# One transposition of the gated product for both token halves in a two-layer encoder on Trainium2

## The chip, the cores and the metric

The kernel runs on one core of one Trainium2 chip. The metric is the device time of one execution in microseconds; three runs stand for the kernel before. The core's engines run side by side, each with its own queue: TensorE (PE, with its weight loads as PEld), VectorE (DVE), ScalarE (ACT), GpSimd (POOL) and SyncE (SP), which issues the DMAs.

## What is computed

One sequence of 256 tokens with 1024 channels goes through two layers in float32. Each layer has two half-step feed-forward blocks around a mixer of three branches:

```python
def swiglu_ffn(h, w_gate, w_up, w_down):
    return (jax.nn.silu(h @ w_gate) * (h @ w_up)) @ w_down
# each layer:
#   x += 0.5 * SwiGLU(RMSNorm(x))                (ffn1)
#   h  = RMSNorm(x); branches S5, GLA, GQA of one input projection of h,
#   each projected to 1024 and weighted by a sigmoid gate from h, then w_out
#   x += merged
#   x += 0.5 * SwiGLU(RMSNorm(x))                (ffn2)
```

The inner width of the feed-forward block is 2816. S5 is a bidirectional state space model over 32 groups, GLA a gated linear attention with four heads, GQA an attention with eight query heads and two key heads.

## The kernel before

**Matrix products.** Tokens are the 128 stationary rows (two halves, `t` = 0 and 1), weights are the moving 512 columns. For precision each float32 operand is split into a high part `hi` and a low part `lo`, and `mm3` issues three matmuls for each k tile of 128: hi by hi (L219), hi by lo (L220), lo by hi (L221). `load` brings weights by DMA into `raw`, two k tiles in one tile; ScalarE copies them to `hi` (L209) and VectorE subtracts to get `lo` (L210). `hi` and `lo` have rings of four, `raw` one of five, and one part feeds 12 matmuls.

**The feed-forward block.** `ffn` has 2816 / 256 = 11 blocks of 256 inner channels. For a block the gate's 256 columns and the up projection's 256 columns make one 512-column bank for each token half; 48 matmuls fill both. Then `evac(b)` is called for t = 0 and t = 1. It applies silu on ScalarE (L294), multiplies on VectorE (L295), and the product, 128 tokens by 256 channels, is transposed on TensorE, since it is the stationary operand of the down projection: two 128x128 transposes (L298) into one PSUM tile `st` of half a bank. ScalarE copies that to the high part `sTh` (L300) and VectorE subtracts to get the low part `sTl` (L301), 128x256 each. `down` then runs over all 22 k tiles of `sTh` and `sTl`. The scratch ring "ra" has four tiles, the PSUM pool `ptr` two banks.

**Stages.** `run` weaves ffn1 of layer 0 with the S5 tables of that layer (`s5_tables`, mostly VectorE), then comes the mixer, then ffn2 of layer 0 and ffn1 of layer 1 in a chain, woven with the tables of layer 1, then the second mixer, ffn2 of layer 1 alone, and the final norm. In the trace these are 0 to 215, 215 to 490, 490 to 895, 895 to 1188 and 1188 to the end.

**The mixer.** The input projection, three gate streams, three branch projections and the merge are TensorE's main work; S5, GLA and attention are side parts woven into it. S5 runs in four quarters: products with an exponential table on VectorE, four scans (L835, L836), products with the run's sums (L349), and TensorE's outputs `yp` (L853, L856). GLA works a head at a time: scores `sp`, masked with a predicated copy (L988), state `kv`, output `go` and its transposition `goT`. Attention works two heads at a time: scores `as` (L1070), softmax on VectorE and ScalarE, transposed probabilities `apt` (L1085) with a copy (L1087), and the product `ao` (L1092). `as`, `yp`, `sp`, `kv` and `ao` share a PSUM ring of three banks.

**What sets the order.** The program is emitted in Python in woven order, with a priority by which weight parts run ahead. The framework then sets the final order of each engine by a timeline of its own at compile time (`schedule_with_timeline_sim=True`), in which every instruction has an assumed duration. Each engine runs its instructions in that fixed order.

Of the kernel before, what the change touches and what calls it, by code (L numbers as in the profile page):

```python
# [9 lines left out]
F32 = mybir.dt.float32  # L10
# [5 lines left out]
P = 128  # L16
D = 1024
KD = D // P
SEQ = 256
# [19 lines left out]
# main steps before a side part begins, and its steps per main step  # L39
# [12 lines left out]
# columns of the constants: those for the mixer, then those for the tables  # L52
# [4 lines left out]
def constants():  # L57
    """Arrays that depend on shapes alone, one row per partition."""
    c = np.zeros((P, C_ALL), np.float32)
    p = np.arange(P)  # L60
    inv = (10000.0 ** (-np.arange(16, dtype=np.float32) * 2.0 / 32)).astype(np.float32)
    for t in range(NT):
        tok = t * P + p
        for blk, pos in ((0, tok // 64), (1, tok % 64)):
            ang = (pos.astype(np.float32)[:, None] * inv[None]).astype(np.float64)
            for half in range(2):
                o = t * 64 + blk * 32 + half * 16
                c[:, C_COS + o:C_COS + o + 16] = np.cos(ang)
                c[:, C_SIN + o:C_SIN + o + 16] = np.sin(ang) * (1 if half else -1)
    c[:, C_MASK:C_MASK + P] = p[:, None] < p[None]  # L70
    c[:, C_TWO:C_TWO + P] = 1 + np.eye(P)
    i = np.arange(SEQ)
    c[:, C_RST:C_RST + SEQ] = i % P != 0
    n = np.arange(64)
    c[:64, C_RM:C_RM + 64] = n != 0
    c[64:, C_RM:C_RM + 64] = n != 63
    q = p % 32
    c[p, C_DM + q] = 1.0
    c[:, C_SGN] = np.where(p < 64, 1.0, -1.0)
    return c  # L80


def cols(*parts):
    """Columns of weights [K, N] side by side: for the k tiles [a, z)."""
    def f(a, z):
        res, o = [], 0
        for w, cs in parts:
            res.append((w[a * P:z * P, cs].rearrange("(k p) n -> p k n", p=P), 0, o))
            o += cs.stop - cs.start
        return res  # L90
    return f


def weave(main, sides, up=nullcontext):
    """Emit main; from its step `start` on, `per` steps of a side part after each step of main.
    sides: list of [start, per, generator]. Whatever is left of them comes in the end."""
    acc = [0.0] * len(sides)
    for i, _ in enumerate(main):
        for j, (start, per, g) in enumerate(sides):
            if i >= start:  # L100
                acc[j] += per
                while acc[j] >= 1.0:
                    acc[j] -= 1.0
                    with up():
                        next(g, None)
    for _, _, g in sides:
        for _ in g:
            pass


def rest(*gens):
    """Emit what is left of these parts, in turn, as one step."""
    gens = list(gens)
    while gens:
        for g in list(gens):
            if next(g, gens) is gens:
                gens.remove(g)
    yield
# [7 lines left out]
class Enc:  # L126
# [38 lines left out]
    def vectors(self, *names, eng=None):  # L165
        """Parameters of channels, to partitions: [128 channels, (layer, tile)]"""
# [26 lines left out]
    def load(self, pieces):  # L193
        """pieces: list of (dram AP [partitions, k tiles, columns], first partition, first column)"""
# [21 lines left out]
    def mm3(self, ps, act, w, first, last):  # L216
        """act: (hi, lo) [128 k, 128 tok]; w: (hi, lo) [128 k, n]"""
# [5 lines left out]
    def stream(self, act, nk, blocks, lead=1):  # L223
        """act(k, t) -> (hi, lo). blocks: list of (pieces(k0, k1) in k tiles, width, evac(t, ps)).
        The first `lead` blocks take their first chunks together."""
# [55 lines left out]
    def ffn(self, l, which):  # L281
        nc, ins = self.nc, self.ins
        wg, wu, wd = (ins[f"{which}_w_{s}"][l] for s in ("gate", "up", "down"))
        with self.tc.tile_pool(name=f"ffn{which}{l}", bufs=1) as fp:
# [5 lines left out]
            def evac(b):  # L290
                def f(t, ps):
                    self.n += 1
                    sg, s = self.t2([P, 256]), self.t2([P, 256])
                    nc.scalar.activation(sg, ps[:, :256], AF.Silu, scale=rstd[:, t:t + 1])  # L294
                    nc.vector.scalar_tensor_tensor(s, ps[:, 256:], rstd[:, t:t + 1], sg, op0=ALU.mult, op1=ALU.mult)  # L295
                    pt = self.ptr.tile([P, 2, P], F32, name=f"st{self.n}", tag="tr")
                    for j in range(2):
                        nc.tensor.transpose(pt[:, j], s[:, j * P:(j + 1) * P], self.ident)  # L298
                    h = sh[:, 2 * b:2 * b + 2, t * P:(t + 1) * P]
                    nc.scalar.copy(h, pt)  # L300
                    nc.vector.tensor_tensor(sl[:, 2 * b:2 * b + 2, t * P:(t + 1) * P], pt, h.bitcast(F32),  # L301
                                            op=ALU.subtract)
                return f
# [57 lines left out]
    def cmul_steps(self, o_re, o_im, a_re, a_im, b_re, b_im, tmp, neg=False):  # L361
        """o = a * b; with neg, o_im is its negative. tmp: four scratch APs"""
# [13 lines left out]
    def horner(self, out, x, cs):  # L376
        """cs from the highest power down"""
# [6 lines left out]
    def reduce_arg(self, r, n, x, inv, parts):  # L384
        """n = nearest integer of x * inv; r = x - n * (sum of parts)"""
# [40 lines left out]
    def s5_params(self, l, c):  # L426
# [68 lines left out]
        # the first four powers, turned back by a chunk  # L495
# [12 lines left out]
        # ef: powers 0 .. 7 of the turn over a chunk; eg: those of its eighth power  # L508
# [130 lines left out]
    def small_tables(self, l, pp):  # L639
        """What the mixer needs apart from its large weights: half the GLA gain, the padded gate weights with the  # L640
        bias as a last row, the rotary tables with the gains of q and k"""
# [36 lines left out]
    def split_into(self, hi, lo, src):  # L678
        """src -> two float32r parts"""
# [68 lines left out]
    def gate_stream(self, l, i, act, rstd, gates):  # L748
        """The tanh of half the gate's argument: sigmoid(v) = (1 + tanh(v / 2)) / 2"""
# [32 lines left out]
    def s5(self, l, m):  # L782
# [18 lines left out]
        for q in range(NQ):  # L801
# [31 lines left out]
            # sums up to the chunk before (forward: after), nothing at the ends  # L833
# [67 lines left out]
    # ---- gate logits: z in two parts against weights in two parts, the products one above the other:  # L901
    # ---- [high z, 1 | high z, 1 | low z] . [high w, high b | low w, low b | high w]
# [18 lines left out]
    # ---- gated linear attention, both directions, a head at a time, over chunks of 128 tokens; the exponents  # L921
# [1 line left out]
    def gla(self, l, m, y):  # L923
# [26 lines left out]
        for h in range(GH):  # L950
# [34 lines left out]
            # a token's own score is the same both ways: forward ones above the diagonal, twice those on it, backward below  # L985
# [113 lines left out]
    def branch(self, l, b, y, gates):  # L1099
        """Generator bodies run late: y[b] is there by then."""  # L1100
# [76 lines left out]
```

## Time and profile before

| | |
|---|---|
| Median of three runs | 1378.79 us (1378.58 to 1380.41) |
| Profiled execution: span | 1376.2 us |
| TensorE busy | 1336.0 us, 97% |
| VectorE busy | 1018.4 us, 74% |
| ScalarE busy | 698.6 us, 51% |
| GpSimd busy | 73.5 us, 5% |

The profiled execution has only its span, 2.6 us under the median of the runs. Busy time counts instructions, not waits; a matmul's listed duration overlaps with the next one's, so the distance from start to start is what one takes of the engine. "[1.27 <-DVE lo L210]" behind a row means that the engine was idle for 1.27 us before it, and that the last thing it waited for was the tile `lo` of line 210 on VectorE.

### The profile page before, as it was taken

To read this page: it belongs to the slowest core of one execution; us is meant where nothing else is said; L and a number is where in the kernel's file an instruction comes from. 1 tells how busy PE (TensorE), PEld (TensorE's weight loads), DVE (VectorE), ACT (ScalarE), POOL (GpSimd) and SP (SyncE) were. 2 spreads that over 40 slices of the span, in tenths; PEclk is the share of its full clock that TensorE was granted. 3 is DMA by queue.
4 is the path that set the end of the run, shared out by engine and by line. 5 is a ranking of instruction groups with operands and counts; after the bars stand their busy time and mean duration, and the time that the engine had idled before them with its cause. 6 is when DMAs were issued, how large, how long until landed. Compare 5 with 4: busy or idle time off the path is not lost.

```text
span 1376.2 us, 19506 instructions
## 1 busy us (share of the span) xinstructions
PE 1336.0 (97%) x6920; PEld 1061.6 (77%) x6920; DVE 1018.4 (74%) x1826; ACT 698.6 (51%) x1102; POOL 73.5 (5%) x104
## 2 busy tenths in 40 slices
PE   7999999999999999999999999999999999999997
PEld 5878788778787678768877777887787877888886
DVE  5899975779986789996465775457799767655553
ACT  5545345447585355445355454354475754555542
POOL 1020210000100000110000000000001000000000
PEclk9999999999999999999999999999999999999999
DMA  7766666565453366666665646566654533655662
GB/s 227 195 211 224 234 222 179 189 205 198 140 183 122 107 161 206 200 202 221 198 195 173 204 149 204 180 178 202 196 200 134 168 107 122 191 178 186 182 213 76
DMA packets 201201, 249.88 MB, mean 182 GB/s; under 512 B 40856, under 2 KB 134600, under 8 KB 201104
## 3 DMA queue, kind: packets, MB, share of 16 engines
q1 hardware_dynamic: 200496, 247.59, 57.5%
q8 instruction: 54, 0.88, 0.3%
q10 hardware_dynamic: 608, 1.06, 0.2%
q14 instruction: 43, 0.35, 0.1%
HBM read 234.44 MB, written 13.11 MB: 180 GB/s over the span
## 4 chain that ended last, share of the span: by engine, by line
PE 63%; issue 17%; DVE 13%; DMA 3%; ACT 3%; POOL 1%; SPq 0%; POOLq 0%; ACTq 0%; DVEq 0%
PE mm L220 18%; PE mm L219 17%; PE mm L221 17%; DVE lo L210 4%; PE S L818 1%; DMA raw<-in_ffn_w_gate 1%; DMA raw<-in_ffn_w_up 1%; PE as L1070 1%; ACT hi L209 1%; PE ao L1092 1%; DVE t L349 1%; PE st L298 1%; DVE run L836 1%; DVE run L835 1%; PE apt L1085 1%
## 5 line engine op out<-in xcount | busy, mean ns | idle before, releaser
L210 DVE TENSOR_TENSOR lo<-raw,hi 128x1024 fp32r<-128x1024 f32 x412 | 499.4, 1217 | 191.7 <-ACT hi L209 184.1
L209 ACT CAST hi<-raw 128x1024 fp32r<-128x1024 f32 x412 | 427.7, 1042 | 305.6 <-PE mm L221 276.3
L220 PE MATMUL mm<-lo,hTh 128*128 128x512 f32 (+1 forms) x1120 | 445.3, 398 | 5.3 <-DVE lo L210 4.9
L219 PE MATMUL mm<-hi,hTh 128*128 128x512 f32 (+1 forms) x1120 | 437.6, 396 | 2.7 <-ACT hTh L267 2.7
L221 PE MATMUL mm<-hi,hTl 128*128 128x512 f32 (+1 forms) x1120 | 436.1, 392 | 0.0
L220 PEld LDWEIGHTS mm<-lo,hTh 128*128 128x128 f32 x1120 | 211.2, 189 | 51.7 <-DVE lo L210 9.2
L219 PEld LDWEIGHTS mm<-hi,hTh 128*128 128x128 f32 x1120 | 211.2, 189 | 45.5 <-ACT hTh L267 3.8
L221 PEld LDWEIGHTS mm<-hi,hTl 128*128 128x128 f32 x1120 | 210.6, 188 | 40.6 <-DVE hTl L268 0.3
L220 PE MATMUL mm<-lo,sThffn 128*128 128x512 f32 x352 | 138.9, 395 | 2.0 <-DVE lo L210 2.0
L221 PE MATMUL mm<-hi,sTlffn 128*128 128x512 f32 x352 | 138.1, 393 | 0.0
L219 PE MATMUL mm<-hi,sThffn 128*128 128x512 f32 x352 | 136.4, 395 | 0.0
L300 ACT CAST sThffn<-st 128x256 fp32r<-128x256 f32 x88 | 32.6, 372 | 128.7 <-PE st L298 128.5
L220 PEld LDWEIGHTS mm<-lo,sThffn 128*128 128x128 f32 x352 | 66.4, 189 | 16.6 <-DVE lo L210 2.5
L221 PEld LDWEIGHTS mm<-hi,sTlffn 128*128 128x128 f32 x352 | 66.5, 189 | 14.1
L219 PEld LDWEIGHTS mm<-hi,sThffn 128*128 128x128 f32 x352 | 66.5, 189 | 13.8
L301 DVE TENSOR_TENSOR sTlffn<-st,sThffn 128x256 fp32r<-128x256 f32 x88 | 36.9, 421 | 50.3 <-ACT sThffn L300 49.9
L294 ACT ACTIVATE t<-mm,rstd 128x256 f32<-128x256 f32 x88 | 41.6, 475 | 43.0 <-PE mm L221 40.2
L295 DVE SCALAR_TENSOR_TENSOR t<-mm,rstd,t 128x256 f32<-128x256 f32 x88 | 41.4, 479 | 12.6 <-ACT t L294 12.4
L818 PEld LDWEIGHTS S<-U,bb 64*128 64x128 f32 x256 | 24.6, 187 | 12.8 <-issue 11.2
L298 PE MATMUL st<-ident,t 128*128 128x128 f32 x176 | 33.4, 272 | 0.0
L298 PEld LDWEIGHTS st<-ident,t 128*128 128x128 f32 x176 | 24.4, 140 | 11.3
L349 DVE TENSOR_TENSOR t<-e,S 128x256 f32<-128x256 f32 x64 | 22.4, 414 | 12.7 <-DMA e<-scr 6.9
(355 smaller groups left out, 1452.6 us busy)
## 6 DMA issues: line engine op xcount, KB each, us to landing
raw<-in_ffn_w_gate SPq DMA_DIRECT2D x176, 256.0 KB, 3.7
raw<-in_ffn_w_up SPq DMA_DIRECT2D x176, 256.0 KB, 4.4
raw<-in_ffn_w_down SPq DMA_DIRECT2D x88, 512.0 KB, 4.6
raw<-in_w_in SPq DMA_DIRECT2D x48, 512.0 KB, 4.4
raw<-in_w_merge_gate SPq DMA_DIRECT2D x48, 512.0 KB, 3.8
raw<-in_w_out SPq DMA_DIRECT2D x16, 512.0 KB, 4.6
scr<-e SPq DMA_DIRECT2D x6, 768.0 KB, 3.7
e<-scr SPq DMA_DIRECT2D x6, 768.0 KB, 5.7
```

Of the source, the lines that this page charges most:

```text
L209: nc.scalar.copy(hi[:, :e - s, :width], raw[:, :e - s, :width])
L210: nc.vector.tensor_tensor(lo[:, :e - s, :width], raw[:, :e - s, :width], hi[:, :e - s, :width].bitcast(F32), op=ALU.subtract)
L219: nc.tensor.matmul(ps, act[0], w[0], start=first, stop=False)
L220: nc.tensor.matmul(ps, act[0], w[1], start=False, stop=False)
L221: nc.tensor.matmul(ps, act[1], w[0], start=False, stop=last)
L294: nc.scalar.activation(sg, ps[:, :256], AF.Silu, scale=rstd[:, t:t + 1])
L295: nc.vector.scalar_tensor_tensor(s, ps[:, 256:], rstd[:, t:t + 1], sg, op0=ALU.mult, op1=ALU.mult)
L298: nc.tensor.transpose(pt[:, j], s[:, j * P:(j + 1) * P], self.ident)
L300: nc.scalar.copy(h, pt)
L301: nc.vector.tensor_tensor(sl[:, 2 * b:2 * b + 2, t * P:(t + 1) * P], pt, h.bitcast(F32), op=ALU.subtract)
L349: self.nc.vector.tensor_tensor(out, a, b, op=ALU.mult)
L818: nc.tensor.matmul(S[g][:, r, a * 64:(a + 1) * 64], bb[rows, a, r], U[rows, pair[a]], start=True, stop=True)
```

## The change

In `evac` the transposes move from each token half to the second call. The first call only makes the gated product of half 0 and keeps it; the second makes that of half 1, issues four transposes into one full bank `[128, 2, 256]`, and splits the whole with one copy and one subtraction of 128x512, by the helper `split_into` that other places use too. The products of both halves live longer: the ring "ra" of four holds silu and product of both halves, exactly a block's. All else in the diff are comments taken out, which shift nothing but three lines of numbering behind `evac`.

```diff
             def evac(b):
+                s = []
+
                 def f(t, ps):
-                    self.n += 1
-                    sg, s = self.t2([P, 256]), self.t2([P, 256])
+                    sg = self.t2([P, 256])
+                    s.append(self.t2([P, 256]))
                     nc.scalar.activation(sg, ps[:, :256], AF.Silu, scale=rstd[:, t:t + 1])
-                    nc.vector.scalar_tensor_tensor(s, ps[:, 256:], rstd[:, t:t + 1], sg, op0=ALU.mult, op1=ALU.mult)
-                    pt = self.ptr.tile([P, 2, P], F32, name=f"st{self.n}", tag="tr")
-                    for j in range(2):
-                        nc.tensor.transpose(pt[:, j], s[:, j * P:(j + 1) * P], self.ident)
-                    h = sh[:, 2 * b:2 * b + 2, t * P:(t + 1) * P]
-                    nc.scalar.copy(h, pt)
-                    nc.vector.tensor_tensor(sl[:, 2 * b:2 * b + 2, t * P:(t + 1) * P], pt, h.bitcast(F32),
-                                            op=ALU.subtract)
+                    nc.vector.scalar_tensor_tensor(s[t], ps[:, 256:], rstd[:, t:t + 1], sg, op0=ALU.mult, op1=ALU.mult)
+                    if t < NT - 1:
+                        return
+
+                    pt = self.ptr.tile([P, 2, SEQ], F32, name=self.nm("st"), tag="tr")
+                    for i in range(NT):
+                        for j in range(2):
+                            nc.tensor.transpose(pt[:, j, i * P:(i + 1) * P], s[i][:, j * P:(j + 1) * P], self.ident)
+                    self.split_into(sh[:, 2 * b:2 * b + 2], sl[:, 2 * b:2 * b + 2], pt)
                 return f
```

`split_into(hi, lo, src)` is `nc.scalar.copy(hi, src)` and `nc.vector.tensor_tensor(lo, src, hi.bitcast(F32), op=ALU.subtract)`.

All orders below are the fixed ones of the compiled programs; numbers behind names only tell tiles apart, and lines of the changed kernel are three higher behind `evac` (L835 is L838, L1070 is L1073).

In ffn2 of layer 0, VectorE, where the tables of layer 1 are worked out: before, twelve rows that end with the `lo` that TensorE waits for at 600.84 (the `lo` ahead of it, lo_5774, is five rows above the first of them).

```order
L373 TENSOR_TENSOR e_6538<-U_6423,U_6424 128x512
L301 TENSOR_TENSOR sTlffn_4915<-st_5682,sThffn_4914 128x2x128
L364 TENSOR_TENSOR T_6533<-bb_7025,lpb 128x512
L365 TENSOR_TENSOR T_6534<-bb_7025,lpb 128x512
L366 TENSOR_TENSOR T_6535<-bb_7025,lpb 128x512
L301 TENSOR_TENSOR sTlffn_4915<-st_5691,sThffn_4914 128x2x128
L368 TENSOR_TENSOR T_6536<-bb_7025,lpb 128x512
L364 TENSOR_TENSOR U_6421<-ef,eg 128x512
L365 TENSOR_TENSOR U_6422<-ef,eg 128x512
L366 TENSOR_TENSOR U_6423<-ef,eg 128x512
L368 TENSOR_TENSOR U_6424<-ef,eg 128x512
L210 TENSOR_TENSOR lo_5835<-raw_5831,hi_5834 128x1024
```

In the changed kernel, VectorE at the same weight parts:

```order
L368 TENSOR_TENSOR U_6356<-ef,eg 128x512
L369 TENSOR_TENSOR U_6357<-ef,eg 128x512
L372 TENSOR_TENSOR e_6472<-U_6355,U_6356 128x512
L684 TENSOR_TENSOR sTlffn_4882<-st_5635,sThffn_4881 128x512
L376 TENSOR_TENSOR e_6472<-U_6357,U_6358 128x512
L210 TENSOR_TENSOR lo_5778<-raw_5774,hi_5777 128x1024
L367 TENSOR_TENSOR U_6355<-ef,eg 128x512
L368 TENSOR_TENSOR U_6356<-ef,eg 128x512
L210 TENSOR_TENSOR lo_5785<-raw_5781,hi_5784 128x1024
L369 TENSOR_TENSOR U_6357<-ef,eg 128x512
L371 TENSOR_TENSOR U_6358<-ef,eg 128x512
L210 TENSOR_TENSOR lo_5832<-raw_5828,hi_5831 128x1024
```

Weight parts stand three rows apart there; the longest stretch without one in these tables now is ten rows, a little further on, and was fifteen before.

In the mixer of layer 0, VectorE at the last quarter of S5: `run` are the scans, t_3461 the GLA's masked scores, and the memsets set the run's ends. Before:

```order
L835 SCALAR_TENSOR_TENSOR run_2589<-e_3338,t_3363 64x511
L836 SCALAR_TENSOR_TENSOR run_2589<-e_3338,t_3363 64x511
L835 SCALAR_TENSOR_TENSOR run_2589<-e_3338,t_3365 64x511
L836 SCALAR_TENSOR_TENSOR run_2589<-e_3338,t_3365 64x511
L349 TENSOR_TENSOR t_3461<-sp_3534,cst 128x256
L1030 TENSOR_REDUCE ass_3464<-t_3472 128x8
L838 MEMSET run_2589 64x16
L839 MEMSET run_2589 64x16
L210 TENSOR_TENSOR lo_3918<-raw_3915,hi_3917 128x1024
L988 COPY_PREDICATED t_3461<-cst,sp_3534 128x256
L349 TENSOR_TENSOR t_3363<-e_3338,run_2589 128x512
L349 TENSOR_TENSOR t_3365<-e_3338,run_2589 128x512
```

After, from the weight part ahead of the scans on (t_3428 are now the masked scores):

```order
L210 TENSOR_TENSOR lo_3891<-raw_3888,hi_3890 128x1024
L1033 TENSOR_REDUCE ass_3431<-t_3436 128x2
L838 SCALAR_TENSOR_TENSOR run_2556<-e_3305,t_3330 64x511
L839 SCALAR_TENSOR_TENSOR run_2556<-e_3305,t_3330 64x511
L838 SCALAR_TENSOR_TENSOR run_2556<-e_3305,t_3332 64x511
L839 SCALAR_TENSOR_TENSOR run_2556<-e_3305,t_3332 64x511
L764 SCALAR_TENSOR_TENSOR gate_1_3726<-mm_3743,rstd_2328,bm_3727 128x512
L210 TENSOR_TENSOR lo_3988<-raw_3985,hi_3987 128x1024
L352 TENSOR_TENSOR t_3428<-sp_3501,cst 128x256
L1033 TENSOR_REDUCE ass_3431<-t_3439 128x8
L956 SCALAR_TENSOR_TENSOR t_3693<-cst,la_3077 128x256
L957 SCALAR_TENSOR_TENSOR t_3693<-cst,la_3077 128x256
```

Before, the next weight part, lo_3918, stood five rows behind the last scan; now lo_3988 stands two rows behind it. The predicated copy followed lo_3918 directly; now it has left this stretch and follows the weight part after lo_3988.

In the mixer of layer 0, TensorE in the attention's tail. Before:

```order
L1092 MATMUL ao_4073<-t_4016,av_2415 64x256
L1092 MATMUL ao_4073<-t_4000,av_2415 64x256
L1092 MATMUL ao_4073<-t_4016,av_2415 64x256
L1070 MATMUL as_4081<-akT_3542,aqT_3541 128x256 x2
L1085 MATMUL apt_4095<-ident,t_4089 128x128 x4
L220 MATMUL mm_4518<-lo_4508,ygh_3108 128x512
L221 MATMUL mm_4518<-hi_4507,ygl_3109 128x512
L219 MATMUL mm_4517<-hi_4513,ygh_3108 128x512
L220 MATMUL mm_4517<-lo_4514,ygh_3108 128x512
L221 MATMUL mm_4517<-hi_4513,ygl_3109 128x512
L219 MATMUL mm_4518<-hi_4513,ygh_3108 128x512
L220 MATMUL mm_4518<-lo_4514,ygh_3108 128x512
```

After, the same stage of attention:

```order
L1095 MATMUL ao_4040<-t_3983,av_2382 64x256
L1095 MATMUL ao_4040<-t_3967,av_2382 64x256
L1095 MATMUL ao_4040<-t_3983,av_2382 64x256
L996 MATMUL kv_4113<-v_2386,la_3077 128x128 x2
L1088 MATMUL apt_4062<-ident,t_4056 128x128 x4
L1003 MATMUL go_4118<-v_2386,t_3944 128x128
L1004 MATMUL go_4118<-gst_4112,t_3933 128x128
L1003 MATMUL go_4118<-v_2386,t_3944 128x128
L1004 MATMUL go_4118<-gst_4112,t_3933 128x128
L1095 MATMUL ao_4192<-t_4067,av_2382 64x256
L1073 MATMUL as_4199<-akT_3509,aqT_3508 128x256 x2
L1088 MATMUL apt_4132<-ident,t_4126 128x128 x4
```

The main matmuls of branch 1 (`mm` with `ygh`) that stood between the links of the attention now come behind all of them; the GLA's `kv` and `go` stand there in their place. The run without main matmuls goes from ao_4040's first to apt_4214, 25 rows.

## Rows read from the trace of the kernel before

**Rows 1.** The page, engine table: busy us, share of span, instructions
```profile
PE 1336.0 (97%) x6920; PEld 1061.6 (77%) x6920; DVE 1018.4 (74%) x1826; ACT 698.6 (51%) x1102; POOL 73.5 (5%) x104
```
**Rows 2.** Windows by stage: from:to, length, busy time (instructions) of each engine, granted clock
```profile
490.00:695.00 205.00, 198.18 (x933) 159.21 (x932) 164.78 (x388) 97.23 (x132) 15.97 (x25) 0.99 0.64 198
695.00:895.00 200.00, 198.87 (x1017) 158.26 (x1017) 124.30 (x165) 95.00 (x134) 7.41 (x13) 1.00 0.58 184
...
1188.00:1377.00 189.00, 179.82 (x810) 147.25 (x808) 100.86 (x118) 87.82 (x117) 0.70 (x1) 0.99 0.53 167
```
**Rows 3.** Waits of PE in 490:695: us in total, times, longest
```profile
PE mm L220 <- DVE lo L210: 3.4, 4, 1.3
PE pt L263 <- DVE t L265: 3.3, 1, 3.3
```
**Rows 4.** Timeline of PE near 149 and 600: start us, us, instruction, [idle, releaser]
```profile
149.43 0.72 PE L220 MATMUL mm<-lo,sThffn 128*128 128x512 f32 x1 [2.04 <-DVE lo L210]
...
599.18 0.39 PE L219 MATMUL mm<-hi,hTh 128*128 128x512 f32 x1
600.84 0.50 PE L220 MATMUL mm<-lo,hTh 128*128 128x512 f32 x1 [1.27 <-DVE lo L210]
```
**Rows 5.** Timeline of DVE from 590 to 600
```profile
590.15 1.22 DVE L210 TENSOR_TENSOR lo<-raw,hi 128x1024 fp32r<-128x1024 f32 x1
...
595.39 0.41 DVE L301 TENSOR_TENSOR sTlffn<-st,sThffn 128x256 fp32r<-128x256 f32 x1
595.72 0.68 DVE L368 TENSOR_TENSOR T<-bb,lpb 128x512 f32<-128x512 f32 x1
596.32 0.68 DVE L364 TENSOR_TENSOR U<-ef,eg 128x512 f32<-128x512 f32 x1
...
599.58 1.21 DVE L210 TENSOR_TENSOR lo<-raw,hi 128x1024 fp32r<-128x1024 f32 x1
```
**Rows 6.** Waits of PE in 215:490, mixer of layer 0
```profile
PE yp L853 <- DVE t L988: 1.4, 1, 1.4
...
PE mm L220 <- DVE lo L210: 0.8, 1, 0.8
...
PE yp L856 <- DVE t L355: 0.4, 1, 0.4
...
PE goT L1014 <- DVE t L1011: 0.2, 1, 0.2
PE apt L1085 <- DVE t L1081: 0.2, 1, 0.2
```
**Rows 7.** Groups by form, all stages: xcount | busy, mean ns | idle before, releaser
```profile
L301 DVE TENSOR_TENSOR sTlffn<-st,sThffn 128x256 fp32r<-128x256 f32 x88 | 36.9, 421 | 50.3 <-ACT sThffn L300 49.9
L298 PE MATMUL st<-ident,t 128*128 128x128 f32 x176 | 33.4, 272 | 0.0
L300 ACT CAST sThffn<-st 128x256 fp32r<-128x256 f32 x88 | 32.6, 372 | 128.7 <-PE st L298 128.5
...
L268 DVE TENSOR_TENSOR hTl<-t,hTh 128x512 fp32r<-128x512 f32 x24 | 15.9, 682 | 0.8 <-ACT hTh L267 0.7
...
L1087 ACT COPY t<-apt 128x512 f32<-128x512 f32 x16 | 9.3, 582 | 9.8 <-PE apt L1085 9.8
```
**Rows 8.** Timeline of DVE in the last feed-forward block, at a block's end
```profile
1273.25 0.48 DVE L295 SCALAR_TENSOR_TENSOR t<-mm,rstd,t 128x256 f32<-128x256 f32 x1 [0.52 <-ACT t L294]
...
1277.45 0.42 DVE L301 TENSOR_TENSOR sTlffn<-st,sThffn 128x256 fp32r<-128x256 f32 x1 [2.04 <-ACT sThffn L300]
```
**Rows 9.** Timeline of PE in the attention tail of the mixer of layer 0
```profile
446.51 1.13 PE L1070 MATMUL as<-akT,aqT 64*128 64x256 f32 x4
447.57 1.08 PE L1092 MATMUL ao<-t,av 128*64 128x256 f32 x6
...
450.71 0.72 PE L1085 MATMUL apt<-ident,t 128*128 128x128 f32 x4 [0.21 <-DVE t L1081]
```

## The prediction

> **What bounds the kernel now.** I read the page's table of engines first: TensorE is busy for 1336.0 of 1376.2 us, 97% [rows 1]. So a saving on another engine is worth nothing unless it ends a wait of TensorE, and TensorE can give back at most the 40 us in which it isn't busy. Then the engines by stage [rows 2]: where the S5 tables of layer 1 are worked out beside a feed-forward block (490 to 695), VectorE is busy for 164.78 of 205 us and TensorE lacks 6.8; in the second half of that stage's chain (695 to 895) TensorE lacks 1.1 of 200; in the last feed-forward block (1188 to 1377) VectorE has only 100.86 of 189. Third, the waits of TensorE: in 490:695 there are 3.4 us in four waits for a low weight half `lo` from VectorE (L210), and 3.3 for the norm's transposes, which the change doesn't touch [rows 3]. The timeline shows how such a wait looks: matmuls start every 0.227 us, and then 599.18 is followed by 600.84, so 1.43 us are lost; the other three waits for `lo` of this stretch look the same, with some 4.0 us lost in all four, and it happens once in layer 0 (2.04 at 149.43) [rows 3, 4]. VectorE explains it: between the `lo` at 590.15 and the one at 599.58 it does 9.4 us of table work and splits with no weight part among it [rows 5], while the ring of four weight parts feeds TensorE for some 4 x 12 x 0.227 = 10.9 us at the very most. In the mixers, three waits cost 1.4 + 0.8 + 0.4 = 2.6 us each time, all for VectorE at the last S5 quarter, and the attention tail another 0.4 [rows 6]; the second mixer repeats them.
>
> **Part 1, fewer and wider instructions.** 88 copies of 0.372 us (L300) become 44 of about 0.582 (a 128x512 copy from the same kind of bank, L1087), and 88 subtractions of 0.421 (L301) become 44 of about 0.682 (L268) [rows 7]. By these durations ScalarE saves 88 x 0.372 - 44 x 0.582 = 7.1 us and VectorE 88 x 0.421 - 44 x 0.682 = 7.0. That flatters it: back to back, the 256-wide subtraction at 595.39 holds VectorE for 0.33 us until the next starts, a 512-wide operation for 0.60 [rows 5]. So the busy VectorE gains 2 x 0.33 - 0.60 = 0.06 us a block, 2.6 us over 44 blocks; 7.0 is the upper end, where no neighbour overlaps. The Trainium skill ("Perfetto Trace Analysis", section "Optimizing Scalar/DVE Operations") gives a fixed cost per VectorE instruction on PSUM of about 125 ns, and says grouping pays if the engine is saturated; as an estimate from that page 44 x 0.125 = 5.5 us of VectorE, against the 2.6 of the rows, and the sum by it would change only in the table stretches.
>
> **Where this lies.** TensorE's own work does not change: 176 transposes before and after, and it never idled ahead of one (0.0 in L298's row) [rows 7]. In the fixed order of the changed kernel the four transposes of a block don't even run together: they stand as two pairs, 5 matmuls apart, 20 or so matmuls behind the end of the block, as before. In the last feed-forward block VectorE waits ahead of its splits anyway (2.04 us at 1277.45), so nothing comes off: 0. The same for 695 to 895: 0. The merged split comes later than the first half's split did by about 1.2 us, but nobody needs it before `down`, whose first k tiles are the first blocks'. There is slack: the gated product of the second half is done at 1273.25 + 0.48, and the first split behind it starts at 1277.45 [rows 8].
>
> **Part 2, the order around it.** The order of each engine is worked out ahead by the framework's own timeline, from durations it assumes. New durations in the feed-forward block therefore shift everything behind, tables and mixers too, and most of my sum comes from there. My measure: between successive `lo` on VectorE I add up VectorE's work (durations from the trace) and subtract TensorE's work between their first uses (0.227 a matmul). Where that difference rises above what the ring has in hand, TensorE waits.
>
> - Tables of layer 1. Before, it rises by 8.6 us and the trace shows 4.0 us lost, so 4.6 were in hand. After, with two table operations between the weight parts where 15 rows stood, it rises by 6.0, leaving 1.4: -2.6 us. Ends: -4.0 (all of it goes) and +2 (one more wait like that at 599.18, whose run moves elsewhere).
> - Tables of layer 0. 3.0 before, 2.7 after: -0.3. Ends -2.0 and +1.
> - Mixers, last S5 quarter. Before, VectorE's four scans and two products stand between weight parts, the difference rises by 10.4 and 2.6 us show as waits [rows 6]. After, weight parts stand right ahead and behind the four scans, it rises by 5.2, and the second `yp`, which waits for the predicated copy, comes 48 matmuls (10.9 us) behind the first instead of 20. I take all three waits as gone: 2 x -2.6 = -5.2. Ends -5.2 and 0.
> - Mixers, attention tail. Scores to transposed probabilities take 3.1 us (the scores that start at 446.51 are done when `ao` starts at 447.57, `apt` starts at 450.71), and a copy of 0.58 lies between `apt` and the products `ao` [rows 7, 9]. Before, main matmuls stand between; they cost 0.4 us of waits [rows 6]. After, `as`, `apt`, `ao` and the GLA's `go` stand in one run of 25 rows with no main matmul. What then lies between falls short by 0.7 and 0.6 (two `ao` right behind their `apt`), 0.4 and 0.2 (two score chains), and 0.5 at `goT`: 2.4, so 2.0 more than before, 2 x 2.0 = +4.0. Ends 0 (short chains hide) and +8 (each link pays a whole copy or semaphore more).
>
> **The sum**: -2.6 - 0.3 - 5.2 + 4.0 = -4.1 us. The profiled span of 1376.2 becomes 1372.1. The median of the runs, 1378.8, lies 2.6 above that span, so I forecast 1374.7 us, -0.3%. About 0.2% (2.8 us) is what a measurement of this kernel can tell from no change.
>
> **Rivals.**
> - Nothing to measure, 1378.8: TensorE is the bound, saved VectorE time is idle time, and the waits that go in the S5 quarter come back in the attention tail one for one (-5.2 against +5 or so). For it: 97% busy, and the zero terms above cover half of the blocks. Against it: four named waits stand just where the order changes.
> - Slower, 1383: the attention tail decides. If each of its links costs a whole copy plus the way between engines (0.58 + 0.5 where I wrote 0.6; the 3.1 us chain bare where I counted part of it), a mixer loses 4 more us than before, +8 for two; if the S5 waits only move one place further (0 instead of -5.2) and the tables give -2.9 still, the sum is about +5. It decides from 3.5 us a mixer in the tail. For it: 25 rows without main work on the engine that sets the time.
> - Faster still, 1370.7: the tail's links hide behind each other and both other terms stand: -8.1.
> - The merged operation hurts. At the end of a block both halves now wait for the second one, and the wide copy and the wide subtraction are 0.21 and 0.26 us longer than the narrow ones [rows 7]. That counts only for the last block ahead of each `down`: 4 x 0.47 = 1.9 us, 1376.6 instead of 1374.7. The 3.7 us between the gated product and its first split [rows 8] speak against it, and so does that TensorE never waits there; I give it 0.04, inside "nothing to measure". The Trainium skill, same page and section, states this as a rule: where VectorE or ScalarE aren't saturated but cause bubbles on other engines, breaking up instructions may let work end sooner. No row of this profile shows such a bubble at the transposes.
> - The change doesn't do what it says. The four transposes land in one bank but are not issued as four; the copies and subtractions do halve. That half of its claim fails costs nothing, since transposes never waited. It changes no case.
>
> **How the numbers follow.** Forecast 1374.7: 0.40. Faster still: 0.11. Nothing to measure: 0.27. Slower: 0.22. The forecast's own terms reach from -8 to 0 around it. The single terms' ends, added, give -11 to +11, but they would all have to fall one way; leaving out about one in ten on each side, and keeping the slower rival inside, I take 1368.5 to 1383.5. Chances: faster by over 0.2% 0.51, within it 0.27, slower 0.22.
>
> **What the profile after would show.** Right: L301's group replaced by 44 subtractions of 128x512 near 0.68 us; no wait for `lo` above 1 us in the table stretch; the wait of `yp` for the predicated copy gone; in the tail, idle TensorE ahead of `apt`, `ao` and `goT` of some 2.4 us. Wrong: if the stretches 695 to 895 and 1188 to 1377 change by more than 0.5 us, something in the feed-forward blocks matters that I count as nothing; if the S5 waits are still there, my measure of the order fails; if the tail idles for more than 4 us a mixer, the slower rival has it.

## The result: the forecast missed, the kernel is 0.5% slower

Over eleven runs each the changed kernel takes 1386.8 us, from 1379.0 to 1392.9, and the kernel before 1378.6, from 1376.7 to 1380.5. The ratio is 1.0053 with a 95% interval of 1.0035 to 1.0071: slower. The forecast was 1374.7 in a range of 1368.5 to 1383.5. The second thing to see is the spread: 14 us from run to run, where the kernel before has 4.

The profiled execution of the changed kernel happened to be its fastest run, 1379.0 us with a span of 1377.2, one microsecond above that of before. From the page and the groups by form, engines and the groups that the change touches ([rows 1, 7] are those of before):

```profile
PE 1335.6 (97%) x6920; PEld 1059.3 (77%) x6920; DVE 1012.8 (74%) x1782; ACT 690.5 (50%) x1058; POOL 90.3 (7%) x104
```
```profile
L630 POOL COPY kx<-ks 128x128 f32<-128x128 f32 x32 | 35.3, 1145 | 223.2 <-DVE ks L613 207.1 <-DMA raw<-in_ffn_w_down 16.2
L304 PE MATMUL st<-ident,t 128*128 128x128 f32 x176 | 33.7, 274 | 2.3 <-DVE t L297 2.3
...
L684 DVE TENSOR_TENSOR sTlffn<-st,sThffn 128x512 fp32r<-128x512 f32 x44 | 30.4, 690 | 59.7 <-ACT sThffn L683 59.7
L683 ACT CAST sThffn<-st 128x512 fp32r<-128x512 f32 x44 | 25.8, 585 | 90.2 <-PE st L304 90.2
```

VectorE is down by 5.6 us and ScalarE by 8.1, TensorE's work is what it was: the change did to the instructions what was worked out. One group in this table had no place in the forecast: GpSimd's copies to `kx` (L630) take 1145 ns each. In the kernel before, the same group reads 613:

```profile
L627 POOL COPY kx<-ks 128x128 f32<-128x128 f32 x32 | 18.3, 613 | 250.5 <-DVE ks L610 250.5
```

TensorE's waits in the stages of [rows 3] and [rows 6], after. In 490:695:

```profile
PE pt L263 <- DVE t L265: 4.0, 1, 4.0
PE st L304 <- DVE t L297: 2.1, 3, 1.0
PE mm L220 <- DVE lo L210: 1.6, 2, 1.0
```

In 215:490:

```profile
PE mm L219 <- DVE gate L764: 1.2, 1, 1.2
...
PE mm L221 <- DVE ysl L900: 0.8, 1, 0.8
PE ao L1095 <- ACT t L1090: 0.7, 1, 0.7
PE goT L1017 <- DVE t L1014: 0.5, 1, 0.5
...
PE go L1003 <- ACT t L1081: 0.2, 1, 0.2
```

The waits for `lo` in the tables of layer 1 fell from 3.4 to 1.6 us, and `yp`, `apt` and the `lo` of the mixers wait no more; in layer 0 the waits for `lo` grew, from 2.0 us in one to 3.2 in six. So most of the waits that the forecast named went, and still the kernel is slower. This profile alone can't say why; one of a longer run can.

### The profile page after: what moved, and what is told of

The parts are those of the page before. It is cut to its first block, busy times and chain, and to the rows that moved or that the text cites. A ratio compares the mean times of both kernels' runs of the same rounds, so it can differ in the third digit from the quotient of the medians.

```text
span 1377.2 us, 19408 instructions
## 1 busy us (share of the span) xinstructions
PE 1335.6 (97%) x6920; PEld 1059.3 (77%) x6920; DVE 1012.8 (74%) x1782; ACT 690.5 (50%) x1058; POOL 90.3 (7%) x104
## 4 chain that ended last, share of the span: by engine, by line
PE 64%; issue 17%; DVE 11%; DMA 4%; ACT 2%; POOL 1%; SPq 1%; POOLq 0%; ACTq 0%; DVEq 0%
PE mm L220 18%; PE mm L221 18%; PE mm L219 18%; DVE lo L210 4%; PE S L821 2%; DMA scr<-e 2%; DMA raw<-in_ffn_w_up 1%; PE ao L1095 1%; PE as L1073 1%; PE st L304 1%; PE yp L859 1%; ACT hi L209 1%; PE pt L263 1%; POOL lpb L507 0%; DVE t L352 0%
## 5 line engine op out<-in xcount | busy, mean ns | idle before, releaser
L684 DVE TENSOR_TENSOR sTlffn<-st,sThffn 128x512 fp32r<-128x512 f32 x44 | 30.4, 690 | 59.7 <-ACT sThffn L683 59.7
L683 ACT CAST sThffn<-st 128x512 fp32r<-128x512 f32 x44 | 25.8, 585 | 90.2 <-PE st L304 90.2
L630 POOL COPY kx<-ks 128x128 f32<-128x128 f32 x32 | 35.3, 1145 | 223.2 <-DVE ks L613 207.1
L821 PEld LDWEIGHTS S<-U,bb 64*128 64x128 f32 x256 | 25.5, 186 | 13.7 <-issue 11.4
```

The source lines that it names most:

```text
L630: nc.gpsimd.tensor_copy(kx[:, :, s], ks.rearrange("p g j f -> p g (j f)")[:, :, (3 - s) * 16:(3 - s) * 16 + 64])
L683: self.nc.scalar.copy(hi, src)
L684: self.nc.vector.tensor_tensor(lo, src, hi.bitcast(F32), op=ALU.subtract)
L821: nc.tensor.matmul(S[g][:, r, a * 64:(a + 1) * 64], bb[rows, a, r], U[rows, pair[a]], start=True, stop=True)
```

## A second profile of the same kernel

> The changed kernel once more, for a profile of another execution: the one profiled first spans 1377.2 us and lies among the fastest of runs from 1379 to 1393 us. If the extra time is a stall that only some executions have (one late transfer or one thin margin, followed by a lower granted clock), runs spread over 10 us or more again, and a profile above 1383 us shows one or two waits of TensorE that the first one lacks. If the extra time is the same shuffle everywhere, the spread is under 4 us and the profile shows many small waits.

Measured: 1385.3 us (1380.1 to 1390.6), ratio 1.0041 (1.0022 to 1.0059). The profiled run took 1384.6 us, span 1382.8. To find the place I set the start of each of the 4896 main matmuls against the same one in the profile of before. The table gives the difference in us at ten of them; a step between two lines is time lost or won in that stretch (columns further right are experiments below):

```
start in before   after  again  only_l0f1  after_kxact
      73.1         -1.3   -0.6    -0.6       -0.7
     169.2         -0.7    0.3     3.3        0.3
     200.0          1.7    8.7     5.9        0.0
     228.1          1.3    8.2     5.5       -0.4
     471.9          0.6    7.5     5.4       -1.2
     599.2          1.3    7.4     6.1       -1.4
     632.3          1.6    7.7     6.3       -3.5
     901.9          1.2    7.3     6.3       -3.0
    1173.5          1.1    6.7     7.3       -3.7
    1367.4          1.0    6.6     7.3       -3.8
```

The two executions of the changed kernel part in one place, between 169 and 200 us, where the tables of layer 0 end beside `down` of ffn1: +2.4 in the one, +8.4 in the other. Behind it they run nearly alike. In `again`, the timelines of TensorE, SyncE's queue and GpSimd there read:

```profile
203.48 0.80 PE L219 MATMUL mm<-hi,sThffn 128*128 128x512 f32 x1 [5.23 <-ACT hi L209]
```
```profile
172.76 6.42 SPq L206 DMA_DIRECT2D raw<-in_ffn_w_down  x3
194.74 3.61 SPq L633 DMA_DIRECT2D scr<-kx  x8
198.45 6.63 SPq L206 DMA_DIRECT2D raw<-in_ffn_w_down  x6
```
```profile
178.03 11.02 POOL L620 TENSOR_TENSOR e<-r,tcst 128x512 f32<-128x512 f32 x1 [9.31 <-DMA scr<-e]
188.99 5.72 POOL L630 COPY kx<-ks 128x128 f32<-128x128 f32 x4
```

Read from below: GpSimd begins one product of the tables (L620, a tile of 128x512) at 178.03 and has it after 11.02 us; only then come its four copies to `kx`. SyncE is to store `kx` (L633), and waits for it from 179 to 194.74. Behind that store stand the next loads of `w_down` in the same queue; they go out from 198.45 on. ScalarE gets its raw weights late, and TensorE stands idle for 5.23 us until 203.48. Behind that idle stretch its clock is down: the matmuls at 203.48 and 204.74 last 0.80 us where 0.39 is usual, and the window from 200 to 210 has a mean granted clock of 0.66, between the two levels of 0.5 (1.2 GHz) and 1 (2.4 GHz) (third number from the right; the first after the length is TensorE's busy time):

```profile
200.00:210.00 10.00, 6.05 (x18) 4.56 (x19) 4.99 (x6) 5.43 (x7) 1.94 (x4) 0.66 1.02 366
```

SyncE's waits in 150:215 name the cause:

```profile
SPq L633 <- POOL kx L630: 24.7, 3, 15.5
```

In the same window of the kernel before, SyncE waits for these copies once, for 1.5 us:

```profile
SPq L630 <- POOL kx L627: 1.5, 1, 1.5
```

In the first profile the same product (178.43) took 1.56 us, and the stores went out at 183.34:

```profile
178.43 1.56 POOL L620 TENSOR_TENSOR e<-r,tcst 128x512 f32<-128x512 f32 x1 [10.71 <-DMA scr<-e]
179.94 3.37 POOL L630 COPY kx<-ks 128x128 f32<-128x128 f32 x4
```

Why 1.56 there and 11.02 here? In the first profile VectorE had just stood idle for 0.60 us, up to 178.40, and GpSimd got in behind its next operation. VectorE paid for it: its `lo` at 179.01 took 2.06 us where 1.22 is usual, and at 185.64, where the +2.4 of this execution arises, TensorE waits 1.95 us for a `lo`.

```profile
179.01 2.06 DVE L210 TENSOR_TENSOR lo<-raw,hi 128x1024 fp32r<-128x1024 f32 x1
```

In `again` VectorE worked without a gap. The product was through only when two additions came whose input `mm` lies in PSUM: it ends at 189.05, 1.00 us behind the start of the first, and its shortest time in this profile is 1.04.

```profile
188.05 1.29 DVE L317 SCALAR_TENSOR_TENSOR x<-mm,x 128x512 f32<-128x512 f32 x2
```

## Which block it is

Each feed-forward block alone gets the merged transposition, the other three keep the old one:

```diff
+            evac = evac2 if (l, which) == (0, "ffn1") else evac1
```

> Merged transposition only in ffn1 of layer 0; the other three feed-forward blocks as before. Theory A (the order in ffn1 of layer 0 with its tables, and the mixer behind it, has a thin margin): spread of 10 us or more and a median of 1384 to 1387 us. Theory B (each of the four blocks costs its quarter): median 1380.6, no wide spread. Theory C (the place lies in layer 1's tables): 1378.6 within 1.5.

> Merged transposition only in ffn2 of layer 0, beside the tables of layer 1. Theory A: 1378.6 within 1.5. Theory B: 1380.6. Theory C: a median of 1383 to 1387 us and a wide spread. By the forecast's own sum, the waits for weight parts in these tables shrink by 2.6: 1376.

> Merged transposition only in ffn2 of layer 1, which runs alone behind both mixers and tables, so that all orders ahead of it are those of before: the price of the fewer, wider instructions by themselves. Theories A and C, and the forecast's own term: 1378.6 within 1. Theory B: 1380.6. A rule that merged work lets its reader wait would show as TensorE idling at the transposes or at the first down matmul, 0.5 us or more.

> Merged transposition only in ffn1 of layer 1, where the tables of layer 1 end. Theory Q: 1379 to 1382, since the queue of SyncE has its kx stores there too, though VectorE is less busy than in layer 0. Theory O: as much as ffn2 of layer 0 alone, 1381.8.

Measured, against the kernel before of the same runs: ffn1 of layer 0 alone 1387.2 us, ratio 1.0060 (1.0041 to 1.0078); ffn2 of layer 0 1381.8, 1.0018 (1.0007 to 1.0029); ffn1 of layer 1 1379.6, 1.0000 (0.9990 to 1.0010); ffn2 of layer 1 1379.5, 1.0005 (0.9994 to 1.0017). The first is as slow as the whole change: theory A, though its four runs spread over 4.6 us and not over 10. For ffn2 of layer 0 theory A's 1378.6 within 1.5 fails: beside the tables of layer 1 the merged block costs 0.18% by itself, and its profile, of its slowest run, shows copies to `kx` of 10.12 us at 595.32 and 4.3 us lost between 599.2 and 632.3. Where a block runs beside no or few tables the merged transposition costs and gives nothing, as forecast (0 for each). In the profile of `only_l0f1` the copies to `kx` took 10.19 us as well:

```profile
144.98 10.19 POOL L647 COPY kx<-ks 128x128 f32<-128x128 f32 x4 [26.57 <-DVE ks L630]
```

Of the 3.9 us that it loses from 73 to 169, 3.4 come at one late load of `w_up`, for which TensorE waits 2.30 us up to 75.23, with matmuls 0.43 us apart behind it; `only_l1f2`, whose order there is that of before, has 3.5 at the same load, so this part need not be the change's.

## Who lets GpSimd in

The same four copies in the two kernels, first the changed one, GpSimd and what VectorE does meanwhile:

```profile
141.01 10.19 POOL L630 COPY kx<-ks 128x128 f32<-128x128 f32 x4 [26.58 <-DVE ks L613]
```
```profile
140.86 0.69 DVE L372 TENSOR_TENSOR e<-U,U 128x512 f32<-128x512 f32 x1
...
148.62 1.23 DVE L210 TENSOR_TENSOR lo<-raw,hi 128x1024 fp32r<-128x1024 f32 x1
149.75 0.69 DVE L684 TENSOR_TENSOR sTlffn<-st,sThffn 128x512 fp32r<-128x512 f32 x1
```

and the kernel before:

```profile
141.71 3.33 POOL L627 COPY kx<-ks 128x128 f32<-128x128 f32 x4 [23.47 <-DVE ks L610]
```
```profile
142.57 0.69 DVE L365 TENSOR_TENSOR U<-ef,eg 128x512 f32<-128x512 f32 x1
143.18 0.42 DVE L301 TENSOR_TENSOR sTlffn<-st,sThffn 128x256 fp32r<-128x256 f32 x1
```

From 140.86 on, VectorE of the changed kernel runs thirteen operations back to back whose two inputs both lie in SBUF. GpSimd's four copies, which take 1.00 us when VectorE rests, are let in only when the split's subtraction (L684), whose one input `st` lies in PSUM, starts at 149.75, and end 1.45 us later. In the kernel before such a subtraction (L301) stands at 143.18, and the copies are done after 3.33 us. The split's subtractions were openings for GpSimd: 88 of them before, 44 now, and in this stretch none for nine microseconds. Other operations of VectorE that read PSUM are openings too, as the additions of L317 were above. Once GpSimd is in, it needs no further one: in the first profile its copies from 179.94 to 183.31 took turns with four VectorE operations of two SBUF inputs, which lasted 0.77 us instead of 0.69.

The Trainium skill ("SBUF — State Buffer", section "Who interferes with whom") has this rule: VectorE and GpSimd share a port pair under an exclusive lock, a VectorE instruction with two SBUF inputs contends with a GpSimd instruction that reads SBUF, and one with at most one SBUF input, outside VectorE's two-port modes, doesn't. The trace agrees, by the rows above. It also shows more than the page's "for the whole instruction": across thirteen instructions in a row GpSimd didn't get in between any two.

To test the openings by themselves, in the kernel before ScalarE copies the transposed product to SBUF too, and VectorE subtracts from that copy:

```diff
+                    pc = fp.tile([P, 2, P], F32, name=f"pc{self.n}", tag="pc", bufs=2)
+                    nc.scalar.copy(pc, pt)
                     nc.scalar.copy(h, pt)
-                    nc.vector.tensor_tensor(sl[:, 2 * b:2 * b + 2, t * P:(t + 1) * P], pt, h.bitcast(F32),
+                    nc.vector.tensor_tensor(sl[:, 2 * b:2 * b + 2, t * P:(t + 1) * P], pc, h.bitcast(F32),
```

> The kernel before with one thing taken away: VectorE's 88 subtractions of the split read no PSUM any more, since ScalarE first copies the transposed product to SBUF as well (88 more copies of some 0.37 us on an engine that is half idle). Theory W (GpSimd gets in when VectorE works from PSUM or stands still, so the split's subtractions are its openings): copies to kx take much longer, a mean over 0.9 us instead of 0.61, with one of 5 us or more in the tables of layer 0, and the time is 1381 to 1388. If those subtractions are no openings: a mean of kx within 0.45 to 0.75 us, and 1378.6 within 1.5, or up to 2 more for ScalarE's copies.

Measured: 1391.9 us (1389.2 to 1395.3), ratio 1.0094 (1.0074 to 1.0113). Its groups, GpSimd's timeline in the tables of layer 1, and the waits of SyncE (100:215) and TensorE (all stages):

```profile
L629 POOL COPY kx<-ks 128x128 f32<-128x128 f32 x32 | 42.9, 1382 | 244.1 <-DVE ks L612 198.4 <-DMA raw<-in_ffn_w_down 45.7
...
L303 DVE TENSOR_TENSOR sTlffn<-pc,sThffn 128x256 fp32r<-128x256 f32 x88 | 37.2, 422 | 57.0 <-ACT sThffn L302 56.6
...
L301 ACT COPY pc<-st 128x256 f32<-128x256 f32 x88 | 32.8, 372 | 122.5 <-PE st L298 122.2
```
```profile
599.37 11.96 POOL L629 COPY kx<-ks 128x128 f32<-128x128 f32 x4 [30.81 <-DVE ks L612]
611.29 9.30 POOL L619 TENSOR_TENSOR e<-r,tcst 128x512 f32<-128x512 f32 x1
```
```profile
SPq L632 <- POOL kx L629: 18.5, 4, 11.1
```
```profile
PE mm L220 <- DVE lo L210: 16.7, 10, 8.3
```

The subtractions are as many and as long as before (88 of 422 ns), only their input moved. The copies to `kx` now take 1382 ns each, SyncE waits 18.5 us for them, and TensorE's waits for `lo` are 16.7 us, where the whole kernel before has 7.0. That is theory W, though the time lies 4 us above its range. One reservation: with the added copies the compile-time order of the table stretches shifted too, most in layer 0 (the mixers' hardly), so the 13 us need not be the openings alone.

At 599 the comparison is clean. Around these copies VectorE's rows are those of the kernel before but for one that changed places with its neighbour. Before, the copies pass with the first subtraction:

```profile
592.67 2.25 POOL L627 COPY kx<-ks 128x128 f32<-128x128 f32 x4 [31.27 <-DVE ks L610]
```
```profile
593.06 0.42 DVE L301 TENSOR_TENSOR sTlffn<-st,sThffn 128x256 fp32r<-128x256 f32 x1
```

In `before_nowin` they pass neither with the same subtraction, now from SBUF, nor with the next at 602.50, but with the gated product of L295, which reads `mm` from PSUM: they end 1.47 us behind its start. From 599.2 to 632.3 this kernel loses 8.4 us.

```profile
599.76 0.42 DVE L303 TENSOR_TENSOR sTlffn<-pc,sThffn 128x256 fp32r<-128x256 f32 x1
...
609.86 0.48 DVE L295 SCALAR_TENSOR_TENSOR t<-mm,rstd,t 128x256 f32<-128x256 f32 x1
```

But not every stall of the changed kernel comes from a missing subtraction. The costly one of `again`, at 178.03, begins 7.7 us behind the start of the last split (170.3; 165.4 in the kernel before, which has none near either). There the change acts by the order: before, the product came at 173.01, ahead of `ks` (L610), which reads `kp` from PSUM at 175.27, and took 3.24 us; in `again` it comes behind `ks`. And the stall at 141 is followed by no loss of more than 1 us in the table up to 169. How much of the cost is missing openings, and how much a shifted order that puts GpSimd's work beside a run without any, isn't separated.

```profile
173.01 3.24 POOL L617 TENSOR_TENSOR e<-r,tcst 128x512 f32<-128x512 f32 x1 [10.98 <-DMA raw<-in_ffn_w_down]
```

## Who waits for GpSimd

Two edits leave the merged transposition as it is. The first lets GpSimd issue the stores of `kx`, so that no weight load stands behind them; the orders of TensorE, VectorE and ScalarE stay row for row. The second makes `kx` on ScalarE; it moves a dozen rows of VectorE's order.

```diff
-                    nc.sync.dma_start(
+                    nc.gpsimd.dma_start(
```

```diff
-                nc.gpsimd.tensor_copy(kx[:, :, s], ks.rearrange("p g j f -> p g (j f)")[:, :, (3 - s) * 16:(3 - s) * 16 + 64])
+                nc.scalar.copy(kx[:, :, s], ks.rearrange("p g j f -> p g (j f)")[:, :, (3 - s) * 16:(3 - s) * 16 + 64])
```

> The changed kernel with one edit: the 64 small stores of the tile kx to DRAM are issued by GpSimd, which makes kx, and no longer by SyncE, where weight loads queue up behind them. The orders of TensorE, VectorE and ScalarE are those of the changed kernel row for row. Theory Q (GpSimd's copies to kx come late because VectorE keeps it out, SyncE waits for them, and the weight loads behind them come late): no wait for weights near 200 us, granted clock full there, runs within 5 us of each other, median 1376 to 1380. Theory O (the order of TensorE and VectorE itself costs the time): 1384 to 1388 as before, spread over 10 us.

> The same edit in the kernel before. Theory Q: little is at stake there, since GpSimd's copies came early enough: 1377 to 1379.5. If it gains as much as the same edit gives the changed kernel (over 4 us), the edit helps for another reason and theory Q isn't shown.

> The changed kernel with the copies to kx on ScalarE instead of GpSimd; their stores stay on SyncE. Theory Q: SyncE's waits for kx fall from 10 us and more to about 1, no wait for weights near 200 us, runs within 5 us, median 1376 to 1380. If only the queue mattered and not who makes the copies, it would stay at 1384 to 1388.

> The changed kernel with kx on ScalarE once more, beside the next one on the same chip: 1374 within 1, ratio 0.995 to 0.997, runs within 3 us.

> The kernel before with the copies to kx on ScalarE. If lateness of GpSimd only costs the changed kernel: 1377 to 1379.5, and the change by itself is then worth some 4 us, as its order was forecast to be. If the kernel before gains as much as the changed one (1373 to 1375), the change is worth nothing by itself and the 12 us between 1386 and 1374 say nothing about it.

Measured:

| kernel | median us | runs us | ratio to before |
|---|---|---|---|
| after_kxq: changed, stores of kx on GpSimd | 1377.8 | 1374.9 to 1381.9 | 0.9985 (0.9975 to 0.9995) |
| before_kxq: before, stores of kx on GpSimd | 1380.6 | 1378.6 to 1382.7 | 1.0008 (0.9998 to 1.0018) |
| after_kxact: changed, kx on ScalarE | 1374.0 | 1373.3 to 1374.6 | 0.9957 (0.9942 to 0.9972) |
| after_kxact2: the same once more | 1374.5 | 1371.1 to 1376.0 | 0.9967 (0.9956 to 0.9979) |
| before_kxact: before, kx on ScalarE | 1377.4 | 1375.0 to 1379.3 | 0.9985 (0.9969 to 1.0001) |

With one queue changed and no order of TensorE, VectorE or ScalarE, some 8 us come off the changed kernel's median; the kernel before gains nothing by that. With this queue in both, on one chip, the change even wins 2.8 us (1377.8 against 1380.6). So theory Q holds and theory O falls: the order of TensorE and VectorE doesn't cost the time by itself, the queue does. (Its runs spread over 7 us, not the 5 that theory Q expected.) With `kx` on ScalarE it is 11 to 13 us, and the time is the forecast's 1374.7 within 0.7. That nearness is partly luck, since the same edit takes some 1.6 us off the kernel before. Theory Q had expected less (1376 to 1380), SyncE's waits for `kx` of about 1 us where 6.6 are left, and for `after_kxact2` a spread of 3 us where it is 4.9. In `after_kxq`, GpSimd's copies are as late as ever (10.19 us at 141.76), and SyncE waits for GpSimd only for the end of the tile `e`, 2.7 us in 100:215 and once in 540:720:

```profile
SPq L627 <- POOL e L620: 4.5, 1, 4.5
```

From 599.2 to 632.3 this kernel loses 1.2 us against before, where `after_kxact` wins 2.1. In `after_kxact` the waits of SyncE for `kx` (100:215) and of TensorE for `lo` (all stages) are:

```profile
SPq L633 <- ACT kx L630: 6.6, 4, 2.3
```
```profile
PE mm L220 <- DVE lo L210: 1.2, 3, 0.5
```

A late GpSimd need cost nothing by itself. The profile of `after_kxact2` is the fastest of all, 1371.1 us, and there the product stalls as long as in `again`; but no store of GpSimd's copies stands behind it, and SyncE's waits of 100:215 name GpSimd nowhere:

```profile
174.32 10.58 POOL L620 TENSOR_TENSOR e<-r,tcst 128x512 f32<-128x512 f32 x1 [7.42 <-DMA scr<-e]
```

The last experiment takes GpSimd's product L620 off it as well:

```diff
-            nc.gpsimd.tensor_tensor(ld["e"][:, SCR_R - SCR_E:].rearrange("p (g c) -> p g c", g=GQ),
-                                    self.r4[:, gs].unsqueeze(2).to_broadcast((P, GQ, 64)),
-                                    self.tab(C_RM, 64).unsqueeze(1).to_broadcast((P, GQ, 64)), op=ALU.mult)
+            er = ld["e"][:, SCR_R - SCR_E:].rearrange("p (g c) -> p g c", g=GQ)
+            for g in range(GQ):
+                nc.scalar.activation(er[:, g], self.tab(C_RM, 64), AF.Copy, scale=self.r4[:, q * GQ + g:q * GQ + g + 1])
```

> As after_kxact, and the last table operation of GpSimd in this stage, the product that fills the end of e (L620 of the changed kernel, 1.0 to 11 us), also on ScalarE, as eight scaled copies. If what is left of GpSimd's lateness still costs something: 1371 to 1373. If it lies beside other work: 1374 within 1; slower than 1375 if ScalarE's 64 more copies push weight parts.

Measured: 1372.8 us (1372.5 to 1375.3), ratio 0.9958 (0.9943 to 0.9973), beside 0.9967 (0.9956 to 0.9979) for `after_kxact2` on the same chip: not told apart. What is left of GpSimd's lateness costs at most a microsecond or two. Both beat the kernel before; the simpler one, the changed kernel with `kx` on ScalarE, was measured 0.43% and 0.33% faster than it.

## Why the prediction was wrong, point by point

- **What bounds the kernel** was read right: TensorE, and the waits for `lo` behind a busy VectorE. It stopped there. The tables have a third engine and a queue, GpSimd and SyncE, and the forecast names neither. (Of the 9.4 us that it reads between two `lo` of VectorE, 1.1 are the first `lo` itself.)
- **Part 1, the instructions**: right in size. 44 x 0.690 and 44 x 0.585 where 0.682 and 0.582 were taken; ScalarE's busy time fell by 8.1 (forecast 7.1), VectorE's by 5.6 (7.0).
- **Part 1, where it lies**: 0 for the two blocks without or with few tables held (1.0005 and 1.0000). What failed is the sentence that nobody needs the half's split at its place but `down`. By its data, that is so. By its place on VectorE, GpSimd needed it: at 141 and 606 us its copies waited some nine microseconds for the next one, and the forecast put that at nothing without looking at GpSimd. With the shifted order the cost came in beside the sum: 11 to 13 us in the median (1385.3 and 1386.8 against 1374.5 and 1374.0), of which some 1.6 are what the same edit gives the kernel before.
- **Part 1, the transposes**: they wait 2.3 us in all, where 0 was forecast. A small miss, in the table stretches only.
- **Part 2, tables of layer 1**: forecast -2.6. In the changed kernel as it stands the stretch from 471.9 to 632.3 gives +1.0 and +0.2 in two profiles; with `kx` on ScalarE it gives -2.3 in one and -2.8 in the other, with -0.1 in the kernel before with that edit. The term was right for what it counted, and GpSimd's copies (10.12 us at 606.62) took it back. They stood beside the very ten rows that were counted as the longest without a weight part (604.58 to 611.28 in the trace); a longer one, of thirteen rows, begins at 589.33.
- **Part 2, tables of layer 0**: forecast -0.3 with ends of -2.0 and +1. The start of 228.1 is +1.3 and +8.2 late; with `kx` on ScalarE it is -0.4 and -2.4, and -1.4 in the kernel before with that edit. Here lies most of the miss, and this step failed: the measure of the order adds up the work of VectorE and TensorE alone. What the runs show in its place is GpSimd kept out for up to 11.02 us, SyncE waiting 15.5 for it, and TensorE idle for 5.23 and then at a lower clock.
- **Part 2, mixers**: -2.6 and +2.0 made -0.6 for each. From 228.1 to 471.9 the first mixer gives -0.7 in both profiles and -0.8 in `after_kxact`; the second, from 901.9 to 1173.5, -0.1, -0.6 and -0.7. The waits for `yp` went; a wait for a gate (1.2) and one for `ysl` (0.8) came; the tail's named waits are 0.7, 0.5 and 0.2 = 1.4, where 2.4 was forecast.
- **The rivals**: the slower one had the sign and, by luck, about the price (1383); its mechanism was wrong, since the tail decides nothing. A link costs less than its 0.58 + 0.5: in the first mixer the copy of `apt` runs from 441.62 for 0.59 us and `ao` starts at 442.25. "Faster still" and "nothing to measure" fell. The merged operation did hurt, but not by the reader's wait of the fourth rival: its last block ahead of `down` costs nothing (`only_l1f2`, 1.0005).
- **The range** was too narrow on the slow side by 3.3 us. Its bounds came from terms on two engines; a third engine's late work has no bound in them.

With `kx` out of GpSimd's hands in both kernels, the change is worth 1374.0 and 1374.5 against 1377.4, some 3 us, by the two ratios on the same chip 0.9967 / 0.9985 = 0.9982. With the stores of `kx` on GpSimd's queue in both, it is 2.8. So the forecast's -4.1 was somewhat too large even for a kernel whose weight loads don't wait behind these copies. What isn't settled: no run above 1385.4 us of the changed kernels was profiled, so the slowest, of 1392, may have a second stall of this kind, in the tables of layer 1 for one.

## What to carry to other kernels

When instructions of VectorE are merged, moved or given another source, look at what GpSimd does at that moment: an operation that reads PSUM may be the only opening through which GpSimd gets to work. Then follow who waits for GpSimd: here 16 KB stores in SyncE's queue, with weight loads of 512 KB behind them, turned a late copy into an idle TensorE. A kernel whose runs spread more than before the change may have such a race in it; profile a second execution and compare the start of the same matmul.

## What the runs showed of the hardware

The granted clock of TensorE fell to 0.50, the lower of its two levels (1.2 of 2.4 GHz), with no idle time ahead of it in the profile. In the second mixer of the changed kernel it ran on without a gap through 64-column matmuls of S5 and 256-column ones of the GLA (993.95 to 997.35, the last L821 x6 at 996.54), and from 997.35 the 512-column ones came 0.43 us apart instead of 0.23 for some 3.5 us. Windows of 2 us there (columns as above), and TensorE's timeline:

```profile
996.00:998.00 2.00, 2.00 (x11) 1.64 (x12) 1.88 (x4) 1.21 (x3) 0.00 (x0) 0.84 0.58 216
998.00:1000.00 2.00, 2.00 (x6) 1.60 (x5) 2.00 (x6) 1.99 (x3) 0.00 (x0) 0.50 0.71 219
1000.00:1002.00 2.00, 2.00 (x8) 1.60 (x7) 1.99 (x3) 1.38 (x2) 0.00 (x0) 0.80 0.11 43
```
```profile
996.54 0.88 PE L821 MATMUL S<-U,bb 64*128 64x64 f32 x6
...
998.37 0.63 PE L219 MATMUL mm<-hi,hTh 128*128 128x512 f32 x1
998.79 0.63 PE L220 MATMUL mm<-lo,hTh 128*128 128x512 f32 x1
...
1001.10 0.40 PE L220 MATMUL mm<-lo,hTh 128*128 128x512 f32 x1
1001.33 0.40 PE L221 MATMUL mm<-hi,hTl 128*128 128x512 f32 x1
```

It happened in some mixers of some executions, with the orders of both kernels (`before_kxq` shows a granted clock of 0.83 from 990 to 1000). It costs little: `again` has it in the first mixer and lacks a wait for a gate of 1.2 us there, which the first profile has, and both come out of that mixer at -0.7.
